# Two-layer encoder trunk on one NeuronCore: the quadrant sums of both gate weights sent one transfer per attention head by GpSimd, and one residual addition moved from GpSimd to VectorE

## Chip, cores, metric

One core of a Trainium2 chip. The time is the device time of one execution in microseconds, the median of three runs. A profile of one execution gives the trace. The engines are named as the profile names them: PE is TensorE's matmul stream and PEld its weight loads, DVE is VectorE, ACT is ScalarE, POOL is GpSimd and SP is SyncE. SPq and POOLq are the transfers that SP and POOL issue; in the profile POOL's transfers belong to the queue called software dynamic and SP's to the one called hardware dynamic.

## The reference

All is float32, 512 tokens of width 1024.

```python
for i in range(2):
    xn = rmsnorm(x, norm_g[i])
    y = mixer_na(xn, ...) if i % 2 == 0 else mixer_mla(xn, ...)
    h = x + y
    gate = sigmoid(rmsnorm(h, ple_norm[i]) @ ple_w_gate[i])
    x = h + gate * (p[i] @ ple_w_proj[i])
return rmsnorm(x, final_norm)
```

The first mixer is neighbourhood attention (16 heads of 64 on a grid 64 wide, with a bias per head), the second multi-head latent attention. Each multiplies its result by a SiLU gate and projects it out. The change touches two places: the preparation of `ple_w_gate` for both layers, which runs during the neighbourhood attention, and the addition `h + gate * (...)` of the first layer.

## The kernel before

**Precision.** A float32 product is made of three fp32r products: each operand is split into a rounded high part and a rest (`whi`/`wlo`, `xh`/`xl`), and high times high, rest times high and high times rest are added in PSUM. For a weight, SP loads the raw piece (`wraw`), ACT copies it to `whi` or `wwhi` (line 83) and POOL subtracts to get `wlo` or `wwlo` (line 84).

**The gate product** of each layer is 512x1024 by 1024x1024, done in `gate_seven` as a 2x2 block product with seven instead of eight block products (lines 568 on). Product `p` needs a weight operand of 256 rows by 1024 (1 MB): a quadrant for p = 1, 2, 3, a sum of quadrants for p = 4, 5, 6, 7. These sums do not depend on activations. They are made by transfers inside DRAM into `self.sums[layer][p]` (line 62): with q1, q2, q3, f the quadrants with their signs, 7 = f + q3, 5 = q1 + f, 6 = q1 + sum 7, 4 = q2 + sum 6. The products run in the order 1, 7, 2, 6, 5, 3, 4, each over two token blocks i = 0, 1 with twelve matmuls of 512 columns per block. Products share PSUM banks: product 5 continues in the bank of product 6 (tag `T`), so its block i starts when ACT has copied product 6's block i away to `s6[i]` (line 655).

**The end of a gate block** is `finish` (lines 595 to 612): ACT takes the sigmoid in place in PSUM, DVE multiplies by the projected embedding `pe` (line 606), and the result is added to the residual `r` (line 608). With `last=False` the product goes to `pe` in SBUF and POOL adds; with `last=True` the product stays in PSUM and DVE adds. In layer 0, `finish` for product 2 (the first quadrant of the output, token blocks 0 and 1) runs with `last=False`. What follows a block, `done` with the square `sq` of the residual on ACT (line 1063), is put on the list `behind` and issued after the next block's sigmoid. ACT's order there is sigmoid of block 0, a copy for X3, sigmoid of block 1, `sq` of block 0, the two `s6` copies of line 655, and the `whi` copies of the last weight.

**The neighbourhood attention** (`na_heads`) runs over eight pairs of heads j. `project(j + 1)` makes queries, keys and, for j + 1 = 4 and 6, the values of the next pairs from `na_qk` and `na_v` weights; `attend(j)` runs `na_head` for the two heads: SP loads the bias (`last_bias`), PE makes scores (lines 353, 354), DVE adds the bias and finds the maximum, ACT takes the exponential, POOL multiplies by the reciprocal sums (line 376, `last_norm`, four instructions a head), PE transposes the result (lines 388, 390), ACT and DVE split it into `ph` and `pl`, PE multiplies by the values (line 402). POOL also makes the gated product of the earlier pair (lines 209, 213).

**The sums of the gate weights** are issued within these pairs, layer 0's during pairs 0 to 3 and layer 1's during pairs 4 to 7. In a group's first pair, right after the second head's bias load, SP issues four plain copies of 1 MB in a row (`sums_begin`, line 522): 7 from f, 5 from q1, 6 from q1, 4 from q2. After the last normalisation of its second pair POOL issues two accumulating transfers of 1 MB (7 += q3 and 5 += f), after the third pair's one (6 += sum 7), after the fourth pair's one (4 += sum 6), all at line 528 with `max_dma_last_dim=1024`.

The order inside each engine is set when the program is built, by a scheduler which goes by its own estimate of durations; `issue_after` pins an instruction behind another. At run time each engine works through its list in order.

## Time and profile before

| | |
|---|---|
| median of 3 runs | 666.92 us (666.82 to 667.32) |
| the profiled execution | 667.25 us, its span 665.4 us |
| mean granted TensorE clock | 0.993 |

The span is the time from the first to the last instruction of the trace. In the profile a row of a timeline has the start, the duration of the row's group, engine, line, operation and tiles, and in brackets the idle time of that engine ahead of it and what ended it. A row of waits has the waiting instruction, the engine and line it waited for, the sum in microseconds, how often, and the longest. A row of DMA issues has the transfer, the queue, the number, the size of each and the median time from issue to landing.

### The profile page before, as it was taken

To read this page: it belongs to the slowest core of one execution; us is meant where nothing else is said; L and a number is where in the kernel's file an instruction comes from. 1 tells how busy PE (TensorE), PEld (TensorE's weight loads), DVE (VectorE), ACT (ScalarE), POOL (GpSimd) and SP (SyncE) were. 2 spreads that over 40 slices of the span, in tenths; PEclk is the share of its full clock that TensorE was granted. 3 is DMA by queue.
4 is the path that set the end of the run, shared out by engine and by line. 5 is a ranking of instruction groups with operands and counts; after the bars stand their busy time and mean duration, and the time that the engine had idled before them with its cause. 6 is when DMAs were issued, how large, how long until landed. Compare 5 with 4: busy or idle time off the path is not lost.

```text
span 665.4 us, 10116 instructions
## 1 busy us (share of the span) xinstructions
PE 651.3 (98%) x3419; PEld 552.2 (83%) x3419; DVE 401.5 (60%) x854; ACT 438.7 (66%) x875; POOL 429.8 (65%) x375
## 2 busy tenths in 40 slices
PE   9999999998999999998999999999999999999994
PEld 6888888986988888886899888888888888888884
DVE  6180365735737526566842723798888876374865
ACT  7671686846767743685645444888979897536955
POOL 0495466875576564688555635695969978436974
PEclk9999999999999999998999999999999999999998
DMA  9949422996538869544633334220121214583524
GB/s 323 344 149 331 157 87 93 203 322 167 135 106 172 170 131 366 167 133 145 232 98 100 129 97 137 84 67 10 56 64 65 65 49 141 173 334 127 163 91 158
DMA packets 42835, 102.18 MB, mean 154 GB/s; under 512 B 4640, under 2 KB 17696, under 8 KB 42656
## 3 DMA queue, kind: packets, MB, share of 16 engines
q1 hardware_dynamic: 34032, 92.36, 41.3%
q0 software_dynamic: 8320, 8.39, 8.3%
q10 hardware_dynamic: 432, 0.79, 0.3%
q8 instruction: 27, 0.44, 0.3%
q14 instruction: 24, 0.20, 0.1%
HBM read 89.99 MB, written 25.17 MB: 173 GB/s over the span
## 4 chain that ended last, share of the span: by engine, by line
PE 89%; DVE 3%; POOL 3%; ACT 2%; issue 2%; DMA 1%; POOLq 0%; ACTq 0%
PE ps_mm L107 35%; PE ps_S L107 13%; PE ps_mm L740 6%; PE ps_T L139 5%; PE ps_O L851 4%; PE ps_T L643 4%; PE ps_T L107 3%; PE ps_O L107 3%; PE ps_T L238 2%; PE ps_O L402 2%; PE ps_mm L643 2%; PE ps_mm L184 2%; PE ps_T L390 2%; PE ps_S L354 1%; PE ps_S L353 1%
## 5 line engine op out<-in xcount | busy, mean ns | idle before, releaser
L84 POOL TENSOR_TENSOR wwlo<-wraw,wwhi 128x1024 fp32r<-128x1024 f32 (+5 forms) x78 | 143.7, 1855 | 84.3 <-ACT wwhi L83 71.6
L83 ACT ACTIVATE wwhi<-wraw 128x1024 fp32r<-128x1024 f32 (+5 forms) x81 | 65.5, 832 | 62.8 <-PE ps_mm L107 23.7
L591 POOL TENSOR_TENSOR wlo<-wraw,whi 128x512 fp32r<-128x512 f32 x56 | 73.9, 1350 | 22.7 <-ACT whi L589 19.5
L836 POOL TENSOR_TENSOR ex<-ex,rc 128x512 f32<-128x512 f32 x64 | 65.9, 1039 | 25.1 <-DVE rc L835 18.2
L834 ACT ACTIVATE ex<-ps_S,mx 128x512 f32<-128x512 f32 x64 | 44.0, 688 | 11.9 <-DVE mx L832 10.8
L96 DVE TENSOR_TENSOR pt_lo<-ps_T,pt_hi 128x512 fp32r<-128x512 f32 x64 | 43.3, 682 | 7.6 <-ACT pt_hi L94 7.3
L832 DVE TENSOR_REDUCE mx<-ps_S 128x1 f32<-128x512 f32 x64 | 43.7, 683 | 6.9 <-PE ps_S L107 6.2
L376 POOL TENSOR_TENSOR ex<-ex,rc 128x128 f32<-128x128 f32 (+1 forms) x64 | 36.1, 625 | 15.7 <-DVE rc L372 15.7
L94 ACT ACTIVATE pt_hi<-ps_T 128x512 fp32r<-128x512 f32 x64 | 37.7, 595 | 4.4 <-PE ps_T L139 4.2
L107 PE MATMUL ps_mm<-xh,wwhi 128*128 128x512 f32 x152 | 40.2, 397 | 0.0
L107 PE MATMUL ps_mm<-xl,wwhi 128*128 128x512 f32 x152 | 38.5, 391 | 0.0
L139 PE MATMUL ps_T<-ident,ex 128*128 128x128 f32 x256 | 38.4, 272 | 0.0
L107 PE MATMUL ps_mm<-xh,wwlo 128*128 128x512 f32 x152 | 38.1, 391 | 0.0
L139 PEld LDWEIGHTS ps_T<-ident,ex 128*128 128x128 f32 x256 | 31.5, 140 | 7.7 <-POOL ex L836 0.4
L107 PEld LDWEIGHTS ps_mm<-xh,wwlo 128*128 128x128 f32 x152 | 28.4, 188 | 6.0
L107 PEld LDWEIGHTS ps_mm<-xl,wwhi 128*128 128x128 f32 x152 | 28.3, 188 | 5.7
L205 DVE TENSOR_TENSOR u<-ps_O,u 64x512 f32<-64x512 f32 x32 | 22.0, 687 | 17.9 <-ACT u L204 17.4
L589 ACT ACTIVATE whi<-wraw 128x1024 fp32r<-128x1024 f32 x28 | 29.2, 1055 | 5.0 <-DMA wraw<-sum 2.6
L209 POOL TENSOR_TENSOR u<-u,z 128x512 f32<-128x512 f32 x16 | 21.3, 1334 | 16.5 <-DVE u L205 8.7
L107 PEld LDWEIGHTS ps_mm<-xh,wwhi 128*128 128x128 f32 x152 | 27.3, 188 | 4.9
L370 ACT ACTIVATE ex<-ex,mx 128x128 f32<-128x128 f32 (+1 forms) x64 | 30.2, 474 | 1.2 <-DVE mx L363 0.5
L643 PE MATMUL ps_T<-whi,X 128*128 128x512 f32 x96 | 27.4, 408 | 2.0 <-ACT s L655 1.8
(432 smaller groups left out, 1847.3 us busy)
## 6 DMA issues: line engine op xcount, KB each, us to landing
wraw<-na_qk SPq DMA_DIRECT2D x16, 512.0 KB, 3.9
wraw<-sum SPq DMA_DIRECT2D x16, 512.0 KB, 3.3
pe<-pe SPq DMA_DIRECT2D x31, 256.0 KB, 6.7
wraw<-gate SPq DMA_DIRECT2D x12, 512.0 KB, 3.4
wraw<-na_v SPq DMA_DIRECT2D x8, 512.0 KB, 3.9
sum<-gate POOLq DMA_DIRECT2D x4, 1024.0 KB, 14.0
sum<-sum POOLq DMA_DIRECT2D x4, 1024.0 KB, 9.9
wraw<-na_o SPq DMA_DIRECT2D x8, 512.0 KB, 4.1
```

The source lines that it names most:

```text
L83: nc.scalar.activation(hi[:, c], raw[:, c], AF.Copy)
L84: f = lambda e, c=c: e.tensor_tensor(out=lo[:, c], in0=raw[:, c], in1=hi[:, c].bitcast(F32), op=ALU.subtract)
L94: self.last_copy = nc.scalar.activation(hi, src, AF.Copy, scale=scale)
L96: nc.vector.tensor_tensor(out=lo, in0=src, in1=hi.bitcast(F32), op=ALU.subtract)
L107: last = self.last_mm = nc.tensor.matmul(out, l, r, start=i == 0, stop=i == n - 1)
L139: self.last_mm = self.nc.tensor.transpose(t[:, i * P:(i + 1) * P], b, self.ident)
L591: nc.gpsimd.tensor_tensor(out=lo[:, o], in0=raw[:, o], in1=hi[:, o].bitcast(F32), op=ALU.subtract)
L643: mm = nc.tensor.matmul(ps, l, r, start=j == 0 and p in banks, stop=j == 11 and p in (2, 3, 4), skip_group_check=True)
L740: self.last_mm = nc.tensor.matmul(PS[key], *terms[i], start=i == 0, stop=i == len(terms) - 1)
L832: nc.vector.reduce_max(mx, sp, axis=AX.X, negate=True)
L834: nc.scalar.activation(ex, sp, AF.Exp, bias=mx, accum_out=sm)
L836: nc.gpsimd.tensor_tensor(out=ex, in0=ex, in1=rc.to_broadcast([P, S]), op=ALU.mult)
```

## The change

The eight SP copies and eight accumulating POOL transfers become sixteen POOL transfers, one after each head's last normalisation. Step i of a group (i = 0 to 7, head 8l + i) does: copy f to 7; add q3 to 7; copy q1 to 5; add f to 5; copy q1 to 6; add sum 7 to 6; copy q2 to 4; add sum 6 to 4. The copies now have the `max_dma_last_dim=1024` of the additions. An addition waits in POOL's queue for the copy of the head before it. The bytes per copy and per addition are the same as before.

In the gate, `finish` for product 2 gets `last=True` in layer 0 as well: DVE multiplies in PSUM and DVE adds to the residual. The order of what follows is kept by the exception for `(0, 0)` and `(1, 0)`, which still go to `behind`.

```diff
-        def attend(j):
+        def attend(j, also):
...
+                with self.tc.issue_after(self.last_norm.ins):
+                    also(e)
...
-            attend(j)
             l, step = divmod(j, 4)
             if step == 0:
-                with self.tc.issue_after(self.last_bias.ins):
-                    self.sums_begin(l)
-            else:
-                with self.tc.issue_after(self.last_norm.ins):
-                    self.sums_add(l, step - 1)
+                self.quarters(l)
+            attend(j, lambda e: self.sum_step(l, 2 * step + e))
...
-        for p, src in ((7, "f"), (5, 1), (6, 1), (4, 2)):
-            nc.sync.dma_start(t[p], w[src])
...
-        for p, src in {0: ((7, q[3]), (5, q["f"])), 1: ((6, t[7]),), 2: ((4, t[6]),)}[step]:
-            self.nc.gpsimd.dma_start(t[p], src, accum_op=ALU.add, max_dma_last_dim=1024)
+    def sum_step(self, layer, i):
+
+        p, src = ((7, "f"), (7, 3), (5, 1), (5, "f"), (6, 1), (6, 7), (4, 2), (4, 6))[i]
+        src = self.sums[layer][src] if src in (6, 7) else self.quarter[layer][src]
+        self.nc.gpsimd.dma_start(self.sums[layer][p], src, accum_op=ALU.add if i % 2 else ALU.bypass, max_dma_last_dim=1024)
...
-            if layer == 0 and last:
+            if layer == 0 and last and (t, n) not in ((0, 0), (1, 0)):
                 after(t, n, o, wd)
...
-                        finish(i, 0, ps, last=layer == 1)
+                        finish(i, 0, ps, last=True)
```

Three places show how the instructions move. The first is POOL's list around heads 3 to 6 (`ex` are the normalisations, four a head; `sum07` is layer 0's sum 7; `wwlo` the rest of a weight; `u` and `ol` the gated product of the pair before). Before:

```order
L376 TENSOR_TENSOR ex_1083<-ex_1083,rc_1086 128x256 x2
L528 DMA sum07_101<-gate 1024x256
L528 DMA sum05_99<-gate 1024x256
L84 TENSOR_TENSOR wwlo_1477<-wraw_1475,wwhi_1476 128x1024
L376 TENSOR_TENSOR ex_1230<-ex_1230,rc_1233 128x128
L376 TENSOR_TENSOR ex_1230<-ex_1230,rc_1233 128x256 x3
L376 TENSOR_TENSOR ex_1287<-ex_1287,rc_1290 128x128
L376 TENSOR_TENSOR ex_1287<-ex_1287,rc_1290 128x256 x3
L528 DMA sum06_100<-sum07_101 1024x256
L209 TENSOR_TENSOR u_1138<-u_1138,z_371 128x512
L213 TENSOR_TENSOR ol0_497<-u_1138,oh0_495 128x512
L376 TENSOR_TENSOR ex_1557<-ex_1557,rc_1560 128x128
```

Now:

```order
L522 DMA sum05_99<-gate 1024x256
L84 TENSOR_TENSOR wwlo_1476<-wraw_1474,wwhi_1475 128x1024
L374 TENSOR_TENSOR ex_1228<-ex_1228,rc_1231 128x128
L374 TENSOR_TENSOR ex_1228<-ex_1228,rc_1231 128x256 x3
L522 DMA sum06_100<-gate 1024x256
L374 TENSOR_TENSOR ex_1286<-ex_1286,rc_1289 128x128
L374 TENSOR_TENSOR ex_1286<-ex_1286,rc_1289 128x256 x3
L522 DMA sum06_100<-sum07_101 1024x256
L209 TENSOR_TENSOR u_1138<-u_1138,z_371 128x512
L374 TENSOR_TENSOR ex_1556<-ex_1556,rc_1559 128x128
L374 TENSOR_TENSOR ex_1556<-ex_1556,rc_1559 128x256
L213 TENSOR_TENSOR ol0_497<-u_1138,oh0_495 128x512
```

The copy q1 to 6 now stands between heads 4 and 5, and the addition of sum 7 to 6, which needs that copy, stands ahead of head 6's normalisations, of which the first two have moved ahead of `ol`.

The second is SP's list at the start of layer 1's group (head pair 4). Before:

```order
L335 DMA bias_1758<-na_bias 128x384
L335 DMA bias_1815<-na_bias 128x384
L522 DMA sum17_105<-gate 16x16384
L522 DMA sum15_103<-gate 16x16384
L522 DMA sum16_104<-gate 16x16384
L522 DMA sum14_102<-gate 16x16384
L82 DMA wraw_1884<-na_v1 128x1024
L82 DMA wraw_1890<-na_v1 128x1024
L82 DMA wraw_2008<-na_qk 128x1024
```

Now:

```order
L333 DMA bias_1758<-na_bias 128x384
L333 DMA bias_1816<-na_bias 128x384
L82 DMA wraw_1882<-na_v1 128x1024
L82 DMA wraw_1888<-na_v1 128x1024
L82 DMA wraw_2006<-na_qk 128x1024
```

The four copies ahead of the weight loads are gone; the loads keep their order.

The third is DVE's list at the gate of layer 0, at the end of product 2 (line 606, now 600, is the multiplication by `pe`; line 602 the residual addition; `X3` an operand of product 3; `s6` the subtraction that follows product 6). Before:

```order
L563 TENSOR_TENSOR b_2936<-b_2936,ps_T_3020 128x512
L606 TENSOR_TENSOR pe_3206<-pe_3206,ps_mm_3098 128x512
L540 TENSOR_TENSOR X3_3232<-b_2936,X3_3232 128x512
L606 TENSOR_TENSOR pe_3228<-pe_3228,ps_mm_3113 128x512
L1064 TENSOR_SCALAR mn_3225<-ss_3224 128x1
L624 TENSOR_TENSOR ps_S_3147<-ps_S_3147,s6_3250 128x512
```

Now:

```order
L557 TENSOR_TENSOR b_2936<-b_2936,ps_T_3020 128x512
L600 TENSOR_TENSOR ps_mm_3098<-pe_3206,ps_mm_3098 128x512
L602 TENSOR_TENSOR r_2641<-r_2641,ps_mm_3098 128x512
L534 TENSOR_TENSOR X3_3232<-b_2936,X3_3232 128x512
L600 TENSOR_TENSOR ps_mm_3113<-pe_3228,ps_mm_3113 128x512
L1058 TENSOR_SCALAR mn_3225<-ss_3224 128x1
L602 TENSOR_TENSOR r_2643<-r_2643,ps_mm_3113 128x512
L618 TENSOR_TENSOR ps_S_3147<-ps_S_3147,s6_3250 128x512
```

The addition of block 0 stands right behind its multiplication on DVE; POOL's list loses the two additions there.

More of the change, by code (lines that the diff above doesn't have):

```diff
@@ L513, in row_scale, with quarters @@
         nc.gpsimd.tensor_scalar(b, m, EPS, None, op0=ALU.mult)
-    def sums_begin(self, layer):
-        nc = self.nc
+    def quarters(self, layer):
         q = lambda n, c: self.a["gate"][layer, n, c:c + 2].rearrange("c p n -> (c p) n")
-        w = self.quarter[layer] = {1: q(0, 0), 2: q(0, 2), 3: q(1, 2), "f": q(1, 0)}
-        t = self.sums[layer]
-        for p, src in ((7, "f"), (5, 1), (6, 1), (4, 2)):
-            nc.sync.dma_start(t[p], w[src])
-    def sums_add(self, layer, step):
-        t, q = self.sums[layer], self.quarter[layer]
-        for p, src in {0: ((7, q[3]), (5, q["f"])), 1: ((6, t[7]),), 2: ((4, t[6]),)}[step]:
-            self.nc.gpsimd.dma_start(t[p], src, accum_op=ALU.add, max_dma_last_dim=1024)
+        self.quarter[layer] = {1: q(0, 0), 2: q(0, 2), 3: q(1, 2), "f": q(1, 0)}
+    def sum_step(self, layer, i):
+        p, src = ((7, "f"), (7, 3), (5, 1), (5, "f"), (6, 1), (6, 7), (4, 2), (4, 6))[i]
+        src = self.sums[layer][src] if src in (6, 7) else self.quarter[layer][src]
+        self.nc.gpsimd.dma_start(self.sums[layer][p], src, accum_op=ALU.add if i % 2 else ALU.bypass, max_dma_last_dim=1024)
     def temp(self, name):
```

## The prediction

> **What bounds the kernel now.** I read the page's busy times first, then the list of PE's waits, then the timelines around the waits that the change touches.

> ```profile
> span 665.4 us, 10116 instructions
> PE 651.3 (98%) x3419; PEld 552.2 (83%) x3419; DVE 401.5 (60%) x854; ACT 438.7 (66%) x875; POOL 429.8 (65%) x375
> ...
> PE ps_T L643 <- ACT s L655: 1.8, 1, 1.8
> PE ps_O L402 <- ACT ph L94: 1.2, 1, 1.2
> ...
> PE ps_S L353 <- ACT da L285: 0.6, 1, 0.6
> ```

> PE is busy for 98% of the span, so the kernel takes as long as PE's list of matmuls plus the few places where PE stands still or runs slowly. The matmuls are the same before and after. So only three things can move the time: PE's idle places that the change removes, the clock, and idle places that it adds. Of the list's longest waits the first, 1.8 us, is at the gate of layer 0; the other two shown, 1.2 + 0.6 us, lie in the neighbourhood attention. The rest is untouched. Whatever PE gains early reaches the end, if the stretch after it holds no other bound:

> ```profile
> 340.00:640.00 300.00, 299.88 (x1582) 254.54 (x1583) 198.20 (x388) 209.76 (x425) 204.81 (x174) 1.00 0.34 110
> ```

> In these 300 us PE (first number after the length) is idle for 0.12 us, with the other engines at 66 to 70%: a shift passes through.

> **The gate's addition.** The timeline of the end of product 2 in layer 0:

> ```profile
> 307.04 0.68 DVE L606 TENSOR_TENSOR pe<-pe,ps_mm 128x512 f32<-128x512 f32 x1
> 307.70 0.64 ACT L598 ACTIVATE ps_mm<-ps_mm,rs 128x512 f32<-128x512 f32 x1
> 307.94 2.96 POOL L608 TENSOR_TENSOR r<-r,pe 128x512 f32<-128x512 f32 x2
> 308.53 0.61 PE L643 MATMUL ps_T<-wlo,X 128*128 128x512 f32 x2
> 309.71 0.63 ACT L1063 ACTIVATE sq<-r 128x512 f32<-128x512 f32 x1 [1.38 <-POOL r L608]
> 310.34 1.07 ACT L655 ACTIVATE s<-ps_T 128x512 f32<-128x512 f32 x2
> 310.97 1.60 PE L643 MATMUL ps_T<-whi,X 128*128 128x512 f32 x4 [1.83 <-ACT s L655]
> 315.41 1.09 PE L643 MATMUL ps_T<-whi,X 128*128 128x512 f32 x4
> 318.16 1.07 PE L643 MATMUL ps_T<-whi,X 128*128 128x512 f32 x4
> ...
> L608 DVE TENSOR_TENSOR r<-r,ps_T x5: 676/686/690, 317.8 to 652.9; 128x512 f32<-128x512 f32 x5
> ```

> The chain is: DVE multiplies until 307.72, POOL adds, ACT sits idle for 1.38 us until that addition is done, squares until 310.34, copies `s6` until 310.97, and only then may product 5 start in that bank. PE had finished product 6 at 309.14 and stands for 1.83 us. The DVE form of the addition takes 0.69 us (median 686 ns; POOL's two take 2.96 us together) and follows its multiplication directly: 307.72 + 0.69 = 308.41. ACT's second sigmoid ends at 308.34, so the square runs from about 308.45 to 309.08, the `s6` copy to 309.71, and PE starts at 309.71 instead of 310.97. **Gain 1.26 us**; 0.57 us of the gap stay. DVE has the room, as the windows show (length, then busy time of PE, PEld, DVE, ACT and POOL, the granted clock, the DMA share, GB/s):

> ```profile
> 309.00:311.00 2.00, 0.17 (x2) 0.03 (x1) 0.34 (x3) 1.28 (x4) 1.91 (x2) 1.00 0.69 206
> 311.60:314.90 3.30, 3.30 (x9) 2.55 (x8) 0.65 (x2) 1.70 (x2) 2.41 (x2) 0.50 0.30 93
> 315.00:318.40 3.40, 3.40 (x17) 2.78 (x16) 2.66 (x6) 2.03 (x4) 2.50 (x3) 1.00 0.38 116
> ```

> DVE is busy for 0.34 of the 2.0 us after 309.0; the second addition (0.69 us) lies there. Had DVE no room, each addition would push its next instruction by 0.69 us. POOL loses two additions, and nobody waits for it there.

> The same windows show the other cost of the gap. Right after it the granted clock is 0.50, then 1.00 again. The twelve matmuls from 310.97 to 315.41 take 4.44 us, the next twelve, to 318.16, 2.75: 1.69 us lost. This half-clock stretch follows the one long gap of PE in this part. With 0.57 us instead of 1.83 I expect it not to come. Bounds: nothing regained, or all 1.69; the waits of 0.6 to 1.2 us in the list above sit where the clock row of their stretch is 1.00 (quoted below), so I take all. **Gain 1.69 us.** [...]

> **The copies that leave SP.** The timeline of SP, ACT and PE around head pair 4, and the landing of the loads (the last number of a DMA row):

> ```profile
> 133.39 2.40 SPq L522 DMA_DIRECT2D sum<-gate  x4
> 139.84 0.33 SPq L82 DMA_DIRECT2D wraw<-na_v  x1
> 154.69 1.06 ACT L83 ACTIVATE wwhi<-wraw 128x1024 fp32r<-128x1024 f32 x1 [8.72 <-PE ps_mm L107]
> 157.02 0.39 PE L353 MATMUL ps_S<-da,s 128*128 128x256 f32 x1 [0.56 <-ACT da L285]
> ...
> wraw<-na_v SPq DMA_DIRECT2D x1, 512.0 KB, 14.8
> wraw<-na_v SPq DMA_DIRECT2D x1, 512.0 KB, 4.3
> wraw<-na_qk SPq DMA_DIRECT2D x1, 512.0 KB, 8.2
> ...
> 75.00:240.00 165.00, 163.21 (x973) 143.69 (x972) 92.97 (x293) 113.15 (x257) 107.20 (x105) 1.00 0.62 156
> ```

> The `na_v` load issued at 139.84, 6.5 us behind four copies of 1 MB, landed 14.8 us later, at 154.64. ACT's copy of that weight starts at 154.69 after 8.72 us of idleness (the releaser that the row names had long been done), and ACT's copies of `da` are queued behind it; PE waits 0.56 us for them and 1.2 us for the next link. The other `na_v` load shown, at 86.0, took 4.3 us; the `na_qk` load at 122.8, with two POOL transfers in flight, 8.2. After the change one or two POOL transfers are in flight at 139.8, not four copies and an addition. With 8.2 us the load lands at 148.0, 6.6 us earlier than now, where 1.8 is needed. Bounds: 0 if it still lands as late, 1.8 in full. I take **1.8 us gained**, as the 8.2 lies far from 14.8. Layer 0's four SP copies, in head pair 0, stand beside no wait in PE's list, and I take nothing for them.

> **The transfers that POOL gains.** Eight more issues and seven or eight waits for a copy of the head before:

> ```profile
> L528 POOL DMA_DIRECT2D sum<-gate x4: 1274/1657/1829, 117.4 to 205.2; - x4
> ...
> ko<-slab_h SPq DMA_DIRECT2D x2, 128.0 KB, 2.3
> wraw<-sum SPq DMA_DIRECT2D x16, 512.0 KB, 3.3
> sum<-gate POOLq DMA_DIRECT2D x1, 1024.0 KB, 8.8
> sum<-sum POOLq DMA_DIRECT2D x4, 1024.0 KB, 9.9
> sum<-gate POOLq DMA_DIRECT2D x1, 1024.0 KB, 16.6
> ...
> 117.43 2.86 POOL L528 DMA_DIRECT2D sum<-gate  x2
> 124.29 1.19 POOL L376 TENSOR_TENSOR ex<-ex,rc 128x256 f32<-128x256 f32 x2 [0.65 <-DVE rc L372]
> 126.29 2.11 POOL L376 TENSOR_TENSOR ex<-ex,rc 128x128 f32<-128x128 f32 x4 [0.81 <-DVE rc L372]
> 129.15 1.30 POOL L528 DMA_DIRECT2D sum<-sum  x1 [0.74 <-DMA sum<-gate]
> 130.35 1.42 POOL L209 TENSOR_TENSOR u<-u,z 128x512 f32<-128x512 f32 x1
> 133.86 2.12 POOL L376 TENSOR_TENSOR ex<-ex,rc 128x128 f32<-128x128 f32 x4
> 137.52 0.27 PE L388 MATMUL ps_T<-ident,ex 128*128 128x128 f32 x1
> ```

> An issue holds POOL for 1.27 to 1.83 us, so eight cost 10.2 to 14.6 us of POOL. POOL is busy for 107.2 of the 165 us of this stage (row above), and the issues alone fit in the 57.8 left. What can hurt is the wait: an addition that waits for its copy holds up the normalisations queued behind it, and PE transposes those. The tightest place is heads 4 to 6, where head 5's end follows head 4's by 2.9 us (125.48 and 128.40). The copy q1 to 6 is issued at about 125.5, the addition after head 5 waits for its landing, and behind it stand the issue (1.30), `u` (1.42) and the first two of head 6's four normalisations (half of 2.12): 3.78 us. PE wants those at 137.5, or 137.3 since two score matmuls have left the list ahead. So the copy must land by 133.5, 8.0 us after its issue; every us later is a us of PE.

> No row shows a plain copy from POOL. From below: 128 KB on SP take 2.3 us and 512 KB 3.3, so 1 MB by the same slope (1.0 us per 384 KB) 4.7: no stall. From above: an addition takes 8.8 alone and 9.9 in the median: stall 1.9. The second of two that were issued together took 16.6: stall 8.6. A copy only writes where an addition also reads its target, but the addition issued at 117.4 may be unfinished at 125.5 (with 8.8 us it lands at 126.2). I take a landing of 8.5, just below the lone addition since the copy moves in the same queue: **loss 0.5 us**. The other heads are further apart, and there I take nothing; the cover is POOL's spare time. [...]

> **Sum.** −1.26 − 1.69 − 1.8 + 0.5 = −4.25 us, from 667.25 (the profiled execution) to 663.0. The median before is 0.33 lower than that execution, so 662.7.

> **Rivals.**
> (a) *The clock dips for another reason than the gap*. For it speaks that the waits of 0.56 and 1.2 us around 157 us left the clock of their stretch at 1.00, so not every gap halves it; against it, that in the 300 us without a gap it stays at 1.00. −1.26 − 1.8 + 0.5 = −2.56: 664.4.
> (b) *The `na_v` load is late anyway*, because POOL's transfers, now spread over all heads, are in flight beside it. For it speaks the 8.2 us load; against, that 6.6 us are in hand. −1.26 − 1.69 + 0.5 = −2.45: 664.5.
> (c) *The stalls on POOL eat the gain*, several heads at 1 to 2 us each, or the change of order costs what it brings. About 666.9.
> (d) *Slower*: the copy waits its turn behind the addition of the heads before and lands like the second of a pair, 16.6 us after issue. POOL holds head 6's normalisations for 8.6 us at this place, PE stands. −4.75 + 8.6 = +3.85: 670.8. It cancels the gain from a landing of 12.75 us on (8.0 + 4.75). For it speaks that 16.6, and that POOL's transfers share one queue; against it, that single additions took 8.8 to 9.9.

> **How the numbers follow.** Forecast 0.48, (a) 0.10, (b) 0.12, (c) 0.10, (d) 0.20. A measurement tells no less than 0.2%, 1.3 us, from no change: faster are the forecast, (a) and (b), 0.70; same is (c), 0.10; slower is (d), 0.20. The likeliest alone spans 661.9 (no stall, and as much again from smaller waits) to 664.3 (1.6 us more stall, a landing of some 10). The range reaches over (a), (b) and (c), from 661.6 to 667.2, and leaves out (d).

> **What would show it.** Right: no wait for ACT `s` above 0.7 us in PE's list, the granted clock at 1.00 throughout the window after it, and twelve matmuls of product 5 in 2.75 us; no waits for `da` and `ph` of pair 4, and the `na_v` load landing within 10 us. POOL's rows of the additions then name a DMA as releaser with at most some 2 us, and PE waits for POOL's `ex` for less than 1 us. Wrong: PE waits for POOL `ex` in sums above 4 us, copies landing 13 us or more after their issue, or a clock at 0.50 in the gate without a gap.

## The result, and the profile after

| | before | after |
|---|---|---|
| median, same session (4 runs each) | 666.87 us (666.04 to 667.32) | 661.65 us (660.85 to 662.28) |
| the profiled execution | 667.25 us, span 665.4 | 660.85 us, span 658.7 |

The ratio is 0.9923 (95% interval 0.9905 to 0.994): the change makes the kernel 5.2 us faster. Run again in two later sessions the ratio was 0.9925 (0.9913 to 0.9936) and 0.9913 (0.9898 to 0.9928). The two profiled executions lie further apart, 6.4 us, since the one of before is 0.4 above its median and the one of after 0.8 below. Two executions of the last session, one of before at 1321.99 us and one of the last kernel at 929.13 us, are far slower than all others and in no figure here.

The clock row of the page before, each digit a fortieth of the span:

```profile
PEclk9999999999999999998999999999999999999998
```

The page of the profile after, its span, busy times and granted clock:

```profile
span 658.7 us, 10121 instructions
PE 647.8 (98%) x3419; PEld 550.8 (84%) x3419; DVE 403.7 (61%) x856; ACT 439.2 (67%) x875; POOL 432.8 (66%) x381
...
PEclk9999999999999999999999999999999999999998
```

All of PE's waits over 0.5 us in it:

```profile
PE ps_T L956 <- PEq L1209: 0.8, 1, 0.8
PE ps_T L637 <- ACT s L649: 0.6, 1, 0.6
```

The 1.8 us wait for `s` has become 0.6, the waits for `da` and `ph` are gone, and the clock row no longer has the 8 in its middle that the gate left before (the one at the end belongs to the last instructions). PE's busy time has fallen as well, by 3.5 us, with the same 3419 matmuls.

The gate of layer 0 in the timeline after:

```profile
303.18 0.69 DVE L600 TENSOR_TENSOR ps_mm<-pe,ps_mm 128x512 f32<-128x512 f32 x1
303.90 0.69 DVE L602 TENSOR_TENSOR r<-r,ps_mm 128x512 f32<-128x512 f32 x1
304.62 0.63 ACT L1057 ACTIVATE sq<-r 128x512 f32<-128x512 f32 x1
305.25 1.06 ACT L649 ACTIVATE s<-ps_T 128x512 f32<-128x512 f32 x2
305.88 1.20 PE L637 MATMUL ps_T<-whi,X 128*128 128x512 f32 x4 [0.56 <-ACT s L649]
308.76 1.07 PE L637 MATMUL ps_T<-whi,X 128*128 128x512 f32 x4
```

and the window that holds the first twelve matmuls of product 5 (columns as in the prediction):

```profile
305.90:308.70 2.80, 2.80 (x12) 2.33 (x13) 1.83 (x3) 2.31 (x3) 1.30 (x2) 1.00 0.72 235
```

VectorE's addition follows its multiplication, ACT's square follows the addition without idling, and PE waits 0.56 us. The twelve matmuls take 2.88 us (305.88 to 308.76) where they took 4.44.

Around heads 4 to 6, the timeline of POOL and the start of head 6's transposes on PE:

```profile
124.66 0.80 POOL L522 DMA_DIRECT2D sum<-gate  x1
126.18 2.12 POOL L374 TENSOR_TENSOR ex<-ex,rc 128x128 f32<-128x128 f32 x4 [0.72 <-DVE rc L370]
132.88 1.31 POOL L522 DMA_DIRECT2D sum<-sum  x1 [4.58 <-DMA sum<-gate]
133.68 1.82 POOL L209 TENSOR_TENSOR u<-u,z 128x512 f32<-128x512 f32 x1
134.93 1.48 POOL L374 TENSOR_TENSOR ex<-ex,rc 128x128 f32<-128x128 f32 x2
137.06 0.27 PE L386 MATMUL ps_T<-ident,ex 128*128 128x128 f32 x1
```

and the DMA issues, with the landing times of the copy issued at 124.66 and of the `na_v` load issued at 141.94:

```profile
sum<-gate POOLq DMA_DIRECT2D x1, 1024.0 KB, 7.7
wraw<-na_v SPq DMA_DIRECT2D x1, 512.0 KB, 5.7
```

POOL stands for 4.58 us until the copy has landed, 7.7 us after its issue. Head 6's first two normalisations end at 136.41, 0.65 us before PE asks for them: a wait of 4.58 us on POOL that no row of PE's list shows.

### The profile page after: what moved, and what is told of

Read it like the earlier page. It is cut to its first block, busy times and chain, and to the rows that moved or that the text cites. A ratio compares the mean times of both kernels' runs of the same rounds, so it can differ in the third digit from the quotient of the medians.

```text
span 658.7 us, 10121 instructions
## 1 busy us (share of the span) xinstructions
PE 647.8 (98%) x3419; PEld 550.8 (84%) x3419; DVE 403.7 (61%) x856; ACT 439.2 (67%) x875; POOL 432.8 (66%) x381
## 4 chain that ended last, share of the span: by engine, by line
PE 91%; DVE 2%; ACT 2%; POOL 2%; issue 1%; DMA 1%; POOLq 0%; ACTq 0%
PE ps_mm L107 35%; PE ps_S L107 13%; PE ps_mm L734 6%; PE ps_T L139 5%; PE ps_O L845 4%; PE ps_T L637 4%; PE ps_T L107 3%; PE ps_O L107 3%; PE ps_T L238 2%; PE ps_O L400 2%; PE ps_S L637 2%; PE ps_mm L637 2%; PE ps_mm L184 2%; PE ps_T L388 2%; PE ps_S L352 1%
## 5 line engine op out<-in xcount | busy, mean ns | idle before, releaser
L83 ACT ACTIVATE wwhi<-wraw 128x1024 fp32r<-128x1024 f32 (+5 forms) x81 | 65.5, 832 | 54.5 <-issue 21.0
L374 POOL TENSOR_TENSOR ex<-ex,rc 128x128 f32<-128x128 f32 (+1 forms) x64 | 35.7, 617 | 14.6 <-DVE rc L370 14.6
L94 ACT ACTIVATE pt_hi<-ps_T 128x512 fp32r<-128x512 f32 x64 | 37.7, 595 | 4.3 <-PE ps_T L139 4.1
L107 PE MATMUL ps_mm<-xh,wwhi 128*128 128x512 f32 x152 | 40.3, 398 | 0.0
L107 PE MATMUL ps_mm<-xl,wwhi 128*128 128x512 f32 x152 | 38.5, 391 | 0.0
L107 PE MATMUL ps_mm<-xh,wwlo 128*128 128x512 f32 x152 | 38.2, 392 | 0.0
L107 PEld LDWEIGHTS ps_mm<-xh,wwlo 128*128 128x128 f32 x152 | 28.3, 188 | 5.9
L107 PEld LDWEIGHTS ps_mm<-xl,wwhi 128*128 128x128 f32 x152 | 28.4, 188 | 5.7
L209 POOL TENSOR_TENSOR u<-u,z 128x512 f32<-128x512 f32 x16 | 21.8, 1360 | 16.0 <-DVE u L205 9.1
L107 PEld LDWEIGHTS ps_mm<-xh,wwhi 128*128 128x128 f32 x152 | 27.3, 189 | 4.7
L107 PE MATMUL ps_S<-ke,qe 96*128 96x512 f32 x96 | 29.1, 408 | 0.3 <-DMA qe<-rl 0.3
## 6 DMA issues: line engine op xcount, KB each, us to landing
sum<-gate POOLq DMA_DIRECT2D x12, 1024.0 KB, 7.8
wraw<-na_qk SPq DMA_DIRECT2D x16, 512.0 KB, 3.3
wraw<-sum SPq DMA_DIRECT2D x16, 512.0 KB, 3.3
wraw<-gate SPq DMA_DIRECT2D x12, 512.0 KB, 3.4
wraw<-na_v SPq DMA_DIRECT2D x8, 512.0 KB, 4.2
sum<-sum POOLq DMA_DIRECT2D x4, 1024.0 KB, 9.0
wraw<-na_o SPq DMA_DIRECT2D x8, 512.0 KB, 3.6
```

The lines of the kernel that those rows point to most:

```text
L83: nc.scalar.activation(hi[:, c], raw[:, c], AF.Copy)
L94: self.last_copy = nc.scalar.activation(hi, src, AF.Copy, scale=scale)
L107: last = self.last_mm = nc.tensor.matmul(out, l, r, start=i == 0, stop=i == n - 1)
```

## The experiments

The theory after the result: the change has two independent gains, the gate's shorter chain and the earlier `na_v` load, and the prediction mis-sized the second. Open were the size of each, what makes the load late, whether the gap really causes the half clock, and how near POOL's wait is to costing time. Ratios are to the kernel before in the same session.

**The gate alone.** The weight sums stay as before; only `finish` changes.

```diff
-            if layer == 0 and last:
+            if layer == 0 and last and (t, n) not in ((0, 0), (1, 0)):
...
-                        finish(i, 0, ps, last=layer == 1)
+                        finish(i, 0, ps, last=True)
```

> The gate part of the change alone; the weight sums are made as before (four copies in a row from SP, additions from POOL). Theory (two independent gains): the gate gives the 1.26 us of the wait for the s6 copy and the 1.69 us of half clock, so about 2.9 us against before (ratio 0.9956); the waits around 157 us and the late na_v load (about 14.8 us to landing) stay. Rival (the half clock is not caused by the gap): only 1.3 us faster, and the granted clock still 0.50 somewhere in the 4 us after product 5 starts.

Measured: 664.75 us against 666.40, ratio 0.9973 (0.9958 to 0.9988), 1.65 us, nearer to the rival's 1.3 than to the theory's 2.9. Yet its profile shows both of the theory's gains at the gate: the wait for `s` is 0.6 us, and the twelve matmuls behind it take 2.86 us (310.18 to 313.04). What is new is a half-clock stretch elsewhere. These are its windows around the wait for the `na_v` load:

```profile
156.41:159.82 3.41, 1.54 (x8) 0.89 (x7) 1.04 (x2) 3.34 (x8) 2.30 (x1) 1.00 0.17 60
159.84:163.23 3.39, 3.39 (x17) 3.20 (x15) 2.70 (x11) 3.38 (x10) 2.33 (x5) 0.50 0.39 143
```

The waits for `da` and `ph`, 0.64 and 1.23 us, lie in one stretch of 3.41 us in which PE is idle for 1.87; the next 3.41 us run at 0.50. In the profiled execution of before the same waits fell into two such stretches, with 1.00 and 0.78 us idle, and were followed by no half clock:

```profile
154.55:157.96 3.41, 2.41 (x11) 1.55 (x9) 0.00 (x0) 3.20 (x5) 2.13 (x1) 1.00 0.62 230
157.97:161.37 3.40, 2.62 (x13) 1.87 (x13) 2.47 (x6) 3.38 (x12) 1.22 (x4) 1.00 0.46 157
```

But the half clock costs little there. The 87 matmuls of this part that take 18.80 us in before (their row stands below, with the copies behind the load) take 18.91 here:

```profile
152.15:171.06 18.91, 17.04 (x87) 14.57 (x87) 11.12 (x31) 13.83 (x30) 11.06 (x10) 0.91 0.70 172
```

So it does not explain the 1.65. The times of before may: of its 22 runs beside this kernel eleven took 665.3 to 666.1 us and eleven 666.7 to 670.8, and the profiled execution of before, at 667.25, would be of the second kind. If only that kind has the half clock at the gate, the median holds about half of its price. The times fit this; no trace of the quicker kind was kept, so it is not shown.

**The weight sums alone.** The change, with the two lines above as they were.

> The weight sums of the change alone; the gate's addition stays on POOL. Theory: the stretch from 150 to 175 us gives about 3.6 us (what the two traces show between the same matmuls), more than the 1.8 us of listed waits, and no PE wait for POOL; so 3.4 to 3.8 us against before (ratio about 0.9945), with the 1.8 us gap and the half clock still in the gate. Rival (the sum as predicted): 1.8 less 0.5, 1.3 us. Together with the gate alone it should add up to the whole change, 5.2 us in the medians (6.4 between the two profiled executions).

Measured: 662.90 us, ratio 0.9945 (0.9925 to 0.9964), 3.5 us: the theory, not the 1.3 of the prediction's sum. With the gate alone this makes 5.15 us, the whole change. The expectation that the half clock would be there was wrong. In the profiled execution the gap is there at full length, but the clock stays at 1.00. PE's timeline:

```profile
307.52 1.19 PE L637 MATMUL ps_T<-whi,X 128*128 128x512 f32 x4 [1.84 <-ACT s L649]
```

and windows along the 3.413 us of the next experiment, counted from the first rise of the clock, which stands in each trace (6.48 us in this one; in before it is at 4.36 and in the gate alone at 6.23, and the half clocks begin at 311.56 and 159.83, 90 and 45 whole windows later):

```profile
303.44:306.85 3.41, 2.24 (x10) 1.50 (x8) 2.14 (x4) 1.77 (x4) 3.41 (x3) 1.00 0.56 184
306.86:310.27 3.41, 2.75 (x12) 2.28 (x13) 1.45 (x3) 2.98 (x6) 1.83 (x2) 1.00 0.52 167
```

So the gap, split 1.17 and 0.66 us over two such windows, was followed by nothing. In before the whole gap lay in one:

```profile
308.15:311.56 3.41, 1.58 (x8) 0.99 (x7) 1.75 (x4) 2.03 (x6) 2.76 (x2) 1.00 0.60 180
311.57:314.97 3.40, 3.40 (x10) 2.62 (x9) 0.68 (x2) 1.73 (x2) 2.48 (x3) 0.50 0.29 92
```

The runs of this kernel differ in the same way: the six with a mean granted clock of 0.995 or 0.996 took 661.92 to 662.90 us, the five with 0.993 or 0.994 took 663.05 to 665.75.

**What makes the clock halve.** Each head of layer 1's attention copies its first exponential tile onto itself four to six times more, so that PE stands still at many moments.

```diff
+            for n in range(4 + h % 3 if qt == 0 else 0):
+                nc.scalar.activation(ex, ex, AF.Copy)
```

> The change, and in layer 1's attention each head's first exponential tile is copied onto itself by ACT four to six more times before PE transposes it (the values stay the same), so that PE stands still once per head for times of up to some 3 us. Theory (the clock is judged in fixed windows of 3.413 us counted from when the full clock first came, and halves for the next window when PE was idle for about half of one): stretches of half clock begin only at whole multiples of 3.413 us from the first rise, each behind a window with 1.5 us or more of idleness, and gaps of 1.2 to 2 us that straddle a window's edge are followed by none. Rival (a gap longer than some length halves the clock by itself): the half clock follows every gap above one length, at a fixed distance behind it, at no common grid.

Measured (one execution, 716.11 us): the half clock begins eight times in this part, at 419.91, 443.81, 471.11, 484.77, 522.31, 546.21, 563.27 and 590.58 us. The differences, 23.90, 27.30, 13.66, 37.54, 23.90, 17.06 and 27.31, are 7, 8, 4, 11, 7, 5 and 8 times 3.413. So in this trace the half clocks begin on one grid of 3.413 us. Windows cut along it:

```profile
467.70:471.11 3.41, 1.46 (x9) 1.29 (x10) 1.20 (x4) 2.45 (x5) 1.04 (x1) 1.00 0.00 0
471.12:474.52 3.40, 3.40 (x12) 2.73 (x11) 2.69 (x5) 2.78 (x7) 1.04 (x1) 0.50 0.01 2
...
505.25:508.65 3.40, 2.18 (x16) 1.85 (x14) 2.26 (x5) 3.40 (x9) 3.04 (x3) 1.00 0.16 39
508.66:512.07 3.41, 2.04 (x13) 1.81 (x14) 1.33 (x3) 1.92 (x4) 1.47 (x2) 1.00 0.00 0
512.08:515.48 3.40, 3.40 (x18) 2.81 (x18) 2.32 (x6) 2.31 (x6) 1.04 (x1) 1.00 0.00 0
...
583.75:587.16 3.41, 1.53 (x6) 0.92 (x6) 2.38 (x6) 3.41 (x8) 2.44 (x3) 1.00 0.03 11
587.17:590.57 3.40, 1.38 (x8) 1.24 (x9) 0.22 (x2) 2.62 (x7) 3.05 (x3) 1.00 0.19 71
590.59:593.98 3.39, 3.39 (x11) 2.73 (x10) 2.07 (x4) 2.22 (x5) 2.90 (x3) 0.50 0.01 2
```

A gap of 2.60 us that straddles the edge at 508.66 leaves 1.22 and 1.37 us idle in the two windows, and no half clock follows. 1.95 us within one window is followed by it. At 583.75 a window with 1.88 us idle is not, and the next one with 2.02 is; in the gate alone above 1.87 was enough. So in these records a half clock followed windows with 1.83 us idle (the gate of before), 1.87, 1.95 and 2.02, and none followed windows with 1.22, 1.37 and 1.88; they give nothing sharper. The rival, a length of gap by itself, falls: 2.60 us brought no half clock, 1.83 in before did.

**What makes the load late.** Three kernels move the copies. In the first, from SP still, but one per second head behind that head's bias load:

```diff
-                with self.tc.issue_after(self.last_norm.ins):
+                with self.tc.issue_after((self.last_norm if e else self.last_bias).ins):
                     also(e)
...
+        if i % 2:
+            self.nc.gpsimd.dma_start(self.sums[layer][p], src, accum_op=ALU.add, max_dma_last_dim=1024)
+        else:
+            self.nc.sync.dma_start(self.sums[layer][p], src)
```

> The whole change, but the eight plain copies go back to SP, one per second head behind that head's bias load, instead of POOL. Theory (what hurt was 4 MB of copies in flight at once beside the na_v load): as fast as the change within 0.7 us, the na_v load of pair 4 landing within 9 us, no wait of PE there. Rival (a copy from SP ahead of a load in SP's own queue is what delays it): the na_v load, which has one copy right ahead of it, lands later than 9 us and part of the 3.6 us is lost again.

Measured: 660.55 us against 666.40, ratio 0.9908 (0.988 to 0.9936). As fast as the change (661.65 us in its first runs; the two were not run side by side), and the load landed in 3.3 us. It does not test the rival: the copy ahead of this load, issued at 125.1, had landed 7.3 us later, long before the load's issue at 139.6. What it tells is that SP may send the copies if they are spread.

In the second, the gate part of the change and a burst of the four copies from POOL:

```diff
-                with self.tc.issue_after(self.last_bias.ins):
-                    self.sums_begin(l)
+                if l == 0:
+                    with self.tc.issue_after(self.last_bias.ins):
+                        self.sums_begin(l)
...
                     self.sums_add(l, step - 1)
+                    if j == 2:
+                        self.sums_begin(1)
...
+            if layer:
+                nc.gpsimd.dma_start(t[p], w[src], max_dma_last_dim=1024)
```

> The gate part of the change, and the sums as before except that layer 1's four copies are issued in a row by POOL behind head 5's normalisation (about 129 us) instead of by SP at 133 us. Theory (4 MB in flight at once): the na_v load at about 140 us still lands late (over 10 us) and PE still loses 2 to 4 us there; no faster than the gate part alone. Rival (SP's own queue): the load lands within 9 us and the kernel is about 3.6 us faster than the gate part alone. A burst holds POOL for about 4 us ahead of head 6, which may cost PE up to 1 us by itself.

Measured: 660.33 us, ratio 0.9905 (0.9877 to 0.9933), 4.4 us faster than the gate alone. Neither expectation holds in full. The load took 10.5 us, late as the theory says, yet PE lost nothing:

```profile
wraw<-na_v SPq DMA_DIRECT2D x1, 512.0 KB, 10.5
```

Issued at 140.47 it landed at 151.0, 3.7 us earlier than the 154.64 of before, and that is enough. The burst from POOL slowed the load less than the one from SP, 10.5 us to landing against 14.8, and what counted was whether the load passed its due time. Here the load landed ahead of the last two of POOL's copies (153.3 and 157.1); in before it landed behind all four of SP's, the last at 152.5. That fits the rival, SP's own queue, but it does not show it, since POOL's copies also went in smaller pieces (packets of 4 KB, SP's in before of 64 KB) and were issued 3.9 us earlier. Which of these makes the difference stays open.

The third is the kernel before, with one thing moved: layer 1's four copies go behind the loads of pair 6.

```diff
+            if j == 5:
+                with self.tc.issue_after(self.last_load.ins):
+                    self.sums_begin(1)
             attend(j)
...
             if step == 0:
-                with self.tc.issue_after(self.last_bias.ins):
-                    self.sums_begin(l)
+                if l == 0:
+                    with self.tc.issue_after(self.last_bias.ins):
+                        self.sums_begin(l)
```

> The kernel before, with one thing moved: layer 1's four SP copies, still in a row and from SP, are issued behind the loads of pair 6 instead of ahead of them. Theory (the late na_v load is the whole loss around 157 us): both na_v loads of about 140 us land within 6 us, the PE waits for da and ph are gone, the stretch 150 to 175 us is some 3.8 us shorter, and the kernel is 3.4 to 3.8 us faster than before, as much as the weight sums of the change alone. Rival (it was POOL's or the additions' timing): less than 1.5 us.

Measured: 663.71 us against 666.76, ratio 0.9959 (0.9945 to 0.9973), 3.05 us: most of the theory's 3.4 to 3.8, and twice the rival's bound. Both loads landed within 3.3 us:

```profile
wraw<-na_v SPq DMA_DIRECT2D x1, 512.0 KB, 3.1
wraw<-na_v SPq DMA_DIRECT2D x1, 512.0 KB, 3.3
```

Between the same 87 matmuls, the window of before and that of this kernel:

```profile
151.70:170.50 18.80, 17.01 (x87) 13.43 (x87) 11.11 (x31) 14.21 (x31) 11.45 (x10) 1.00 0.72 178
```

```profile
151.63:166.50 14.87, 14.87 (x87) 13.06 (x87) 10.42 (x31) 11.64 (x27) 9.69 (x10) 1.00 0.91 320
```

3.93 us are gained there. Of these 1.79 were idle in the list of waits (18.80 less 17.01); the other 2.14 lay in stretches that count as busy, where the matmuls stood further apart. That the medians show 3.05 and not 3.93 goes in part with the clock: seven of its eleven runs were granted 0.993 on average and took 663.5 to 664.7 us, the two fastest 0.995 and 0.996 and took 662.0 and 662.1. Two runs fit less well, 663.73 at 0.996 and 666.31 at 0.992. The gate's gap is still in this kernel, and most of its runs probably pay for it; where the clock fell in them no trace shows.

**How near POOL's wait is.** The change, with copies in pieces of a quarter of the size, so that they land later. All engines keep their order.

```diff
-accum_op=ALU.add if i % 2 else ALU.bypass, max_dma_last_dim=1024)
+accum_op=ALU.add if i % 2 else ALU.bypass, max_dma_last_dim=1024 if i % 2 else 256)
```

> The change with the eight plain copies cut into pieces of 256 bytes (4096 of them instead of 1024), so that they land later; the order on every engine is the same. Theory (PE has 8.0 us from the issue of the copy behind head 4 before it waits for head 6's normalisations, each further us costs PE one): with a landing of 12 to 20 us PE waits there for POOL for 4 to 12 us, and the kernel is slower than the change by about as much, with smaller waits at other heads. Rival (POOL's waits lie beside other work in any case): under 1 us slower.

Measured: 663.77 us (ratio 0.9963, 0.9948 to 0.9979) beside 661.25 for the change in the same session, 2.5 us slower. A copy of the change goes in 256 packets of 4 KB; a quarter of that is 1 KB, not the 256 bytes of the expectation. The copies landed later by less than I had expected, but each part of the chain shows. The landing:

```profile
sum<-gate POOLq DMA_DIRECT2D x1, 1024.0 KB, 9.2
```

and the timeline of POOL and PE:

```profile
134.78 1.31 POOL L522 DMA_DIRECT2D sum<-sum  x1 [6.00 <-DMA sum<-gate]
...
137.81 0.33 PE L386 MATMUL ps_T<-ident,ex 128*128 128x128 f32 x1 [0.43 <-POOL ex L374]
139.95 0.35 PE L400 MATMUL ps_O<-ph,vt 128*128 128x192 f32 x1 [0.67 <-DVE u L205]
```

The copy behind head 4 landed 9.2 us after its issue instead of 7.7, the addition started at 134.78 instead of 132.88, and PE's next output product (line 400) at 139.95 instead of 138.05: 1.9 us later on PE for 1.9 us on POOL. The rival falls. The profiled execution, at 662.40 us, is one of the faster ones (the ten runs go from 661.98 to 666.27) and only 0.9 above the profiled one of the change beside it (661.54), so more than half of the 2.5 us between the medians is not traced to a place.

**A gap that is left.** The squares of the first quadrant go behind product 5's sigmoid.

```diff
-            while behind and (o or wd == S):
+            while behind and not hold and (o or wd == S):
...
-                        finish(i, 0, ps, last=True)
+                        finish(i, 0, ps, last=True, hold=layer == 0)
```

> The change, and in layer 0's gate the squares of the first quadrant's two blocks are issued behind product 5's sigmoid instead of between the sigmoids of product 2 and the s6 copies. Theory (the remaining gap of 0.56 us ahead of product 5 is ACT's square standing ahead of the s6 copy): the gap goes, 0.5 to 0.6 us faster than the change. Rival (the copy is late for another reason, or the squares block product 5's own chain later): no gain, or a new wait of PE behind 310 us.

Measured: 660.19 us (659.84 to 661.32), ratio 0.9913 (0.9899 to 0.9928), beside 661.25 (661.12 to 661.54) for the change. The wait ahead of product 5 is gone from its list:

```profile
PE ps_T L956 <- PEq L1209: 0.8, 1, 0.8
PE ps_O L400 <- DVE u L205: 0.6, 1, 0.6
PE ps_mm L107 <- ACT x1h L94: 0.3, 1, 0.3
```

The medians lie 1.1 us apart, and two of its six runs are as slow as the change's. Between the profiled executions of the two PE gains 0.8 us at the gate, and 0.4 near 520 us, where the change's list has a wait of 0.5 us (PE `ps_S` for DVE `vt`) that this one's lacks. The edit does not touch that place, and the other two profiles of the change have a wait of only 0.3 and 0.4 there, so this part is taken for chance.

**The change again**, in both later sessions.

> The changed kernel unaltered, beside the others on one chip. 660.9 to 662.3 us as in its first runs, ratio to before 0.992; no half clock between the start and the last 10 us.

> The changed kernel unaltered, beside these two on one chip: 661.2 us.

Measured 661.25 us (661.12 to 661.54) and 660.94 us (660.46 to 661.53). Neither profile has a half clock ahead of the last 10 us. The first one's list of PE's waits has a row that the first profile of the change did not have:

```profile
PE ps_O L400 <- DVE u L205: 0.7, 1, 0.7
```

Its timeline tells where that comes from:

```profile
136.31 0.63 ACT L212 ACTIVATE oh<-u 128x512 fp32r<-128x512 f32 x1 [3.35 <-POOL u L209]
138.09 0.68 DVE L205 TENSOR_TENSOR u<-ps_O,u 64x512 f32<-64x512 f32 x1 [0.46 <-ACT u L204]
138.83 0.35 PE L400 MATMUL ps_O<-ph,vt 128*128 128x192 f32 x1 [0.66 <-DVE u L205]
```

The addition started at 133.65 here, 0.8 us later than in the first profile. Behind it on POOL stands `u`; ACT's `oh` waits 3.35 us for `u`, ACT's next copies and DVE's sum of the head's halves are late with it, and PE cannot reuse the output bank: line 400 starts at 138.83 instead of 138.05. In the second one's profile the copy landed in 7.6 us and there is no such wait. It was through `u` and ACT, not through the normalisations, that POOL's wait first reached PE here.

**Both kinds of edit together**: copies one per second head from SP, squares later.

> Two edits to the change together: the eight plain copies from SP, one per second head, and the squares behind product 5's sigmoid. If the two are independent, 0.7 and 1.0 us below the change, about 659.6 us; if both only took away the same chance of a half-clock stretch or the same wait at head 6, no faster than the better one alone, 660.2.

Measured: 659.63 us, ratio 0.9891 (0.9875 to 0.9908), beside 660.94 for the change in the same session. Its five runs (659.32 to 659.73) lie wholly below those of the change (660.46 to 661.53): 1.3 us better than the change, about as much as the limit of what this measurement tells, and 7.1 better than before. It is the fastest version here. No trace of these five runs was kept, so the waits in them are not seen.

## Why the prediction was right, and where its sizes were off

It forecast 662.7 us in a range of 661.6 to 667.2; 661.65 was measured, 1.05 below the forecast and just inside the range. The direction was right, and both gains came from where it looked for them. That the total came so near is partly luck: the late load gave about twice its term (3.05 us in medians, 3.93 between profiles), the two terms of the gate in the medians little more than half of theirs (1.65 of 2.95).

| term | forecast | measured | from |
|---|---|---|---|
| wait for `s` in the gate | −1.26 | −1.27 (1.83 to 0.56) | profile after |
| half clock | −1.69 | −1.56 between the two profiles (4.44 to 2.88); with the term above only 1.65 in the medians of the gate alone | profile after, gate alone, sums alone, made gaps |
| late `na_v` load | −1.8 | −3.93 between profiles; −3.05 and −3.5 in medians | copies behind the load, sums alone |
| POOL's waits | +0.5 | 0 in two profiles, +0.66 in a third | profile after, the change again |
| sum | −4.25 | −5.2 in the medians; −6.4 between the profiled executions, −6.7 between their spans | |

Between the two spans the account closes: 1.27 and 1.56 us at the gate, and 3.91 in the part with the late load, where the same 86 matmuls take 19.21 us in before and 15.30 after.

**The gate's wait** followed the chain to a hundredth: DVE's row gave the addition, ACT's order the rest.

**The half clock.** The step "With 0.57 us instead of 1.83 I expect it not to come" held: no profile of the change has it. But the size was taken as if every run of before paid it there, and the 1.65 us of the gate alone speaks against that. In these records a gap of 2.60 us split over two windows (1.22 and 1.37) was followed by no half clock and one of 1.83 within one window was, and the windows lay differently in each execution, with the first rise at 4.36, 6.23 and 6.48 us. With the sums alone and with the copies behind the load the gap of 1.84 and 1.82 us was there and the clock of the profile stayed at 1.00; in the gate alone the waits of the attention brought a half clock instead, which cost 0.1 us. Rival (a), in which the dip has another cause, was wrong in its letter and right in its doubt that "not every gap halves it". The argument that the waits around 157 us left the clock alone rested on the luck of that execution's windows, which split them into 1.00 and 0.78 us.

**The late load** is the step that was mis-sized. "Gain 1.8" took the two rows of the list of waits, 0.56 and 1.23, for the whole. The same stretch lost 2.14 us more, in matmuls that start a little later one after the other, behind ACT's `ph`, DVE's `la`, `lb` and `pl` and POOL's `ex`, and that the profile counts as busy; the move of the copies alone showed 3.93. The move also took away the waits behind which the gate alone had its half clock.

**POOL.** The landing was put at 8.5 us and the bound at 8.0; the landing was 7.7 in the first profile and 8.4 and 7.6 in the change again, with 0.66 us of wait at 8.4 and none listed at the other two, and with the smaller pieces, at 9.2, an addition 1.9 us later made PE 1.9 us later. So the bound lay near 7.7 here. The step named the wrong victim: "behind it stand the issue, `u` and the first two normalisations" is true, but ACT's wait for `u` bites first: an addition 0.77 us later made line 400 0.78 us later, while the normalisations still had 0.65 us to spare in the profile after.

One sign was not met: the additions were to wait for a DMA "with at most some 2 us", and this one waited 4.58. The prediction's own figures gave more: with head 5 done at 128.40 and a landing at 134.0 the wait is 5.6. Three of its figures were off as well, without weight in the sum. The 8.8 us of the addition "alone" are those of the first of a pair issued 0.8 us apart; two with no other in flight took 9.0 and 9.1, and the one issued at 117.43 landed at 128.85, not at 126.2. No stall "and as much again from smaller waits" makes 661.7, not 661.9.

Rival (d) had the right place, and the copies landed well short of its 12.75 us. Rival (b) fell: the load landed in 5.7 us. Rival (c) fell with the sums alone.

## What to carry to other kernels

A late load can cost more than the waits that a list shows, here 3.93 us for 1.79: compare the time between the same matmuls in two executions, or count matmuls per window, before a stall is priced. Bulk transfers which nobody needs soon belong behind the loads that are due, or spread out (here the load landed in 3.1 us ahead of them, in 5.7 with them spread, in 14.8 behind four in a row), and the load's due time tells how much company it can bear. A half-clock stretch is to be priced by its chance and by its place, 1.56 us at the gate and 0.1 beside the late load: it pays to cut such a gap even where one profile shows no dip. Cut from 1.83 to 0.56 us here, it was followed by none in any profile of the change; left at 1.8, by one in the profile of before and by none in two others.

## What the runs showed of the hardware that was not expected

```profile
305.31:308.72 3.41, 1.77 (x8) 1.47 (x9) 1.45 (x3) 3.03 (x6) 1.83 (x3) 1.00 0.62 213
308.73:312.10 3.37, 3.37 (x17) 2.77 (x16) 1.95 (x4) 1.90 (x5) 3.37 (x3) 1.00 0.16 43
```

With the made gaps four of the eight half-clock stretches lasted for a second window, one of them after a first window with 1.28 us idle, below, and one after 0.39 (from 484.77); after 0.50 (from 522.31) it did not, and what decided it is not shown:

```profile
443.81:447.21 3.40, 2.12 (x7) 1.92 (x8) 0.34 (x1) 1.79 (x3) 0.00 (x0) 0.50 0.29 77
447.23:450.63 3.40, 3.40 (x11) 2.73 (x10) 2.18 (x5) 1.86 (x5) 1.04 (x1) 0.50 0.00 0
```

In the profile after, a copy of 1 MB from POOL landed in 5.2 to 6.1 us with no addition in flight and in 7.7 to 8.4 with one; an addition took 8.9 to 10.7. Pieces a quarter of the size raised the copy behind head 4 by only 1.5 us (7.7 to 9.2).
